# Differential attention: second score product over all 128 rows, with the causal mask as extra rows of it

## The chip, the cores and the metric

One core of one Trainium2 chip. The metric is the device time of one execution in microseconds (us). A core has five engines with instruction queues of their own: TensorE (PE, matrix products; its weight loads are listed apart, as PEld), VectorE (DVE), ScalarE (ACT), GpSimd (POOL) and SyncE (SP), whose queue issues nearly all loads here.

## The reference, cut to what matters

The kernel computes a two-layer encoder trunk for 512 positions and a model width of 1024. The first layer's mixer has two parts side by side, a Mamba-2 scan and a differential attention; only the latter is touched. Eight heads, each with two query/key pairs of width 64, rotary positions, and a block-causal mask of chunks of 64:

```
CHUNK = 64
def chunk_causal_mask(start, seq_len):
    qi = start + jnp.arange(Q_BLOCK, dtype=jnp.int32)
    kj = jnp.arange(seq_len, dtype=jnp.int32)
    return (kj[None, :] // CHUNK) <= (qi[:, None] // CHUNK)
...
    def block(start, q1b, q2b):
        mask = chunk_causal_mask(start, s)
        p1 = masked_softmax(jnp.einsum('bqhd,bkhd->bhqk', q1b, k1, preferred_element_type=F32) * scale, mask)
        p2 = masked_softmax(jnp.einsum('bqhd,bkhd->bhqk', q2b, k2, preferred_element_type=F32) * scale, mask)
        return jnp.einsum('bhqk,bkhe->bqhe', p1 - lam * p2, vf)
```

A block of 128 queries (Q_BLOCK) holds two chunks. Of the keys up to its own end, only one square is masked: the first 64 queries of a block may not see the last 64 keys of it.

## The kernel before, in words

Activations lie transposed, features on the 128 partitions and the 512 positions along the free axis. Every matrix is cut into *units* of 128 output features with up to 1024 inputs. A unit's weights come from HBM on SP's queue (line 157), are split into a rounded high part (ACT, line 169) and the rest (DVE, line 170), both fp32r, and PE adds three products per 128 inputs (lines 178 to 180): 24 products of 128x512 for a full unit, each with a weight load. The raw weights, the split weights and the PSUM tiles of a tag have two buffers each. `drive` (line 244) goes through a list of items, units and small steps; before it computes a unit it prepares the weights of the next.

The order of the list is written out by hand in `even` (lines 886 to 932): the projection dt, then B/C, then x with the rotary tables in steps between (`rope_step`), z with the scan (`pair`), and then the attention. For each head hd the list holds units q, k and v, and between them four stages of the head before: `stage(n)` (line 906) does `flip` of the step two back, `attend` of the step three back and `scores` of step n, where a step is one query block of one head in the order 3, 2, 1, 0 (512, 384, 256, 128 key columns). For odd heads the order is v, stage, stage, q, stage, k, stage; for even heads q, stage, k, stage, stage, v, stage. So the keys of an odd head are followed by one stage and the q unit of the next head before they are scored, those of an even head by more. For heads 4 to 7 a unit of the output projection is put in. During heads 0 and 1 the end of the scan runs beside it: `gate_norm`, `gate_row`, and eight times `gate_split` (line 724: DVE at line 725, ACT at 729, GpSimd at 730).

The list is not the order on the engines: when the program is built, a scheduler of the framework orders the instructions of each engine from it and places the waits. An instruction that depends on nothing can be put far ahead, and products of one unit can stand between those of another step. On the chip each engine then goes through its queue in that fixed order.

`rope` (line 762) turns a projection into rotated q or k on DVE and ACT. `ev_q` (line 776) makes `qa[c]` for component c = 0, 1: the 64 rows `R[c]` hold q rounded to fp32r, the other 64 rows the remainder. `ev_k` (line 787) makes `k1[c]`, the rounded k in both halves, and `k2`, the remainder of k, in the rows `R[c]` of one tile. `scores` (line 800) then takes three products per component: line 812 over 128 rows (rounded q and its remainder, both against rounded k), line 813 over the 64 rows `R[c]` (rounded q against the remainder of k), and line 814 with one row in bf16 (`mrow` against `nrow`, set up in lines 392 to 396), which adds -1e30 to the last 64 columns for the first 64 queries. DVE takes the row maximum (line 815), ACT the exponential with its sum (line 816).

Other names in the text: `k2` (two buffers) also serves as fifth scratch tile of the rotary tables (line 507); `eb0`, `eb1` belong to `pair` and later to `flip` and `attend`; `vt` (two buffers) holds values of heads (line 744).

Of the kernel before, what the change touches and what calls it, by code (L numbers as in the profile page):

```python
# [9 lines left out]
F32 = mybir.dt.float32  # L10
F32R = mybir.dt.float32r
# [7 lines left out]
P = 128  # L19
T = 512  # L20
# [7 lines left out]
NEG = -1.0e30  # L28
# [93 lines left out]
class Trunk:  # L122
# [356 lines left out]
    def even(self, E):  # L479
        nc, a = self.nc, self.a  # L480
        V, A, G, PE = nc.vector, nc.scalar, nc.gpsimd, nc.tensor
# [3 lines left out]
        sp = ssp = None  # L485

        def t2(tag, dt=F32, bufs=None):
            return self.t(sp, [P, T], tag, dt, bufs)

        def sm(tag, w=64, dt=F32, bufs=None):  # L490
            return self.t(ssp, [P, w], "s_" + tag, dt, bufs)
# [7 lines left out]
        def first_norm():  # L499
            E["st"] = self.first_squares([t2(x) for x in ("hs00", "hs01", "hs02", "hs10", "hs11", "hs12", "fx0",  # L500
                                                          "fx1")])
            E["mask"] = sm("mask", P)
            nc.sync.dma_start(out=E["mask"], in_=a["mask"])
            self.norm_done(E)
            self.rope = {n: self.t(self.cp, [P, T], "rope_" + n) for n in ("cos", "sin")}
            tq = [t2("qa0", F32R if i == 2 else F32, 2) for i in range(2)]
            tq += [t2("qa1", F32R if i == 0 else F32, 2) for i in range(2)] + [t2("k2", bufs=2)]
            E["rope"] = self.rope_tables(self.rope["cos"], self.rope["sin"], self.cst("if64"), self.cst("sg64"), tq, True)

        def rope_step():  # L510
# [223 lines left out]
        vt, qs, ks = [None] * 8, [None] * 8, [None] * 8  # L734
# [38 lines left out]

        R = (slice(0, 64), slice(64, 128))

        def ev_q(hd):
            def f_(ps):
                r = rope(ps, 0.125)
                qa = [t2(f"qa{c}", F32R, 2) for c in range(2)]
                for c in range(2):  # L780
                    A.copy(out=qa[c][R[c], :], in_=r[R[c], :])
                    V.tensor_tensor(out=qa[c][R[1 - c], :], in0=r[R[c], :], in1=qa[c][R[c], :].bitcast(F32),
                                    op=ALU.subtract)
                qs[hd] = qa
            return f_

        def ev_k(hd):
            def f_(ps):
                r = rope(ps, 1.0)
                k1 = [t2(f"k1{c}", F32R, 2) for c in range(2)]  # L790
                k2 = t2("k2", F32R, 2)
                for c in range(2):
                    A.copy(out=k1[c][R[c], :], in_=r[R[c], :])
                    A.copy(out=k1[c][R[1 - c], :], in_=r[R[c], :])
                    V.tensor_tensor(out=k2[R[c], :], in0=r[R[c], :], in1=k1[c][R[c], :].bitcast(F32),
                                    op=ALU.subtract)
                ks[hd] = (k1, k2)
            return f_

        def scores(hd, qb):  # L800
            qa, (k1, k2) = qs[hd], ks[hd]
            if qb == 3:
                W["ss", hd] = sm("ss", 8, bufs=2)
            ss = W["ss", hd]
            n = (qb + 1) * P
            qsl = slice(qb * P, (qb + 1) * P)
            nm = sm("nmx", 2, bufs=2)
            pp = W["pp", hd, qb] = [t2(((("md1", "xs7"), ("hs12", "pp1")) if hd > 2 else (("md1", "fx0"), ("fx1", "pp1")))[c][qb % 2])
                                    for c in range(2)]
            for c in range(2):  # L810
                ps = self.ps("sc")
                PE.matmul(ps[:, :n], lhsT=qa[c][:, qsl], rhs=k1[c][:, :n], start=True, stop=False)  # L812
                PE.matmul(ps[:, :n], lhsT=qa[c][R[c], qsl], rhs=k2[R[c], :n], start=False, stop=False)  # L813
                PE.matmul(ps[:, n - 64:n], lhsT=self.mrow, rhs=self.nrow, start=False, stop=True)
                V.tensor_reduce(out=nm[:, c:c + 1], in_=ps[:, :n], axis=AX.X, op=ALU.max, negate=True)
                A.activation(out=pp[c][:, :n], in_=ps[:, :n], func=AF.Exp, bias=nm[:, c:c + 1],
                             accum_out=ss[:, 2 * qb + c:2 * qb + c + 1])
            rr = sm("rr", 1, bufs=2)
            V.reciprocal(out=rr, in_=ss[:, 2 * qb + 1:2 * qb + 2])
            V.scalar_tensor_tensor(out=rr, in0=ss[:, 2 * qb:2 * qb + 1], scalar=E["nlam"], in1=rr, op0=ALU.mult,  # L820
                                   op1=ALU.mult)
            V.scalar_tensor_tensor(out=pp[0][:, :n], in0=pp[1][:, :n], scalar=rr, in1=pp[0][:, :n], op0=ALU.mult,
                                   op1=ALU.add)
# [62 lines left out]
        L = lambda f, *x: (lambda: f(*x))  # L886
        mt = ("mm", "sc")
        ux = self.units("x", 8, xs8, ev_xbc)
        items = [start] + self.units("dt", 1, xs8, ev_dt, tags=mt) + [first_norm]
        items += self.units("bc", 4, xs8, ev_xbc, 1, tags=mt, j0=8)  # L890
        rs = rope_step
        items += ux[:2] + [L(bc_work, 0), rs] + ux[2:3] + [rs] + ux[3:4] + [L(bc_work, 1), rs]
        items += ux[4:5] + [rs] + self.weave(ux[5:], [L(make_xdt, 0, 0), rs] + [L(make_xdt, 0, c) for c in (1, 2, 3)])
        items += [lambda: self.run(E["rope"])]
        uz = self.units("z", 8, xs8, ev_z)
        for i in range(8):
# [643 lines left out]
def pack(i):  # L1540
    i = {k: np.asarray(v) for k, v in i.items()}
    f = np.float32
    par = np.zeros((P, NPAR), f)

    def put(n, v):
        o, w = PAR[n]
        par[:v.shape[0], o:o + w] = v
    put("nm0", _cols(i["norm_mix"][0]))
    put("nm1", _cols(i["norm_mix"][1]))
    put("nf0", _cols(i["norm_ffn"][0]))  # L1550
    put("nf1", _cols(i["norm_ffn"][1]))
    put("nfin", _cols(i["norm_final"]))
    put("gn", _cols(i["ev_gate_norm"][0]))
    put("cw", _cols(i["ev_conv_w"][0]))
    put("cb", _cols(i["ev_conv_b"][0]))
    put("dsk", _cols(np.repeat(i["ev_d_skip"][0], 64)))
    put("sub", _cols(i["ev_subln"][0]))
    put("lam", i["ev_lambdas"][0].T)
    put("qn", _cols(i["od_q_norm"][0]))
    put("kn", _cols(i["od_kv_norm"][0]))  # L1560
    put("bglu", _cols(i["od_b_glu"][0]))
    put("lre", _cols(i["od_lam_re"][0]))
    put("lim", _cols(i["od_lam_im"][0]))
    put("lst", _cols(np.repeat(i["od_log_step"][0], 64)))
    put("d4", np.tile(i["od_d_skip"][0].reshape(16, 32).T, (4, 1)))
    cst = np.zeros((P, NCST), f)

    def putc(n, v):
        o, w = CST[n]
        cst[:, o:o + w] = v  # L1570
    r = np.arange(P)
    putc("ident", np.eye(P))
    mask = (r[:, None] <= r[None, :]).astype(f)
    cidx = np.ascontiguousarray(np.broadcast_to(r[None, :], (P, P))).astype(f)
    if64 = (10000.0 ** (-np.arange(32) * (2.0 / 64))).astype(f)
    if32 = (10000.0 ** (-np.arange(16) * (2.0 / 32))).astype(f)
    putc("if64", if64[r % 32][:, None])
    putc("if32", if32[r % 16][:, None])
    tp = f(2.0 * math.pi)
    putc("sg64", np.where(r % 64 < 32, -tp, tp)[:, None])  # L1580
    putc("sg32", np.where(r % 32 < 16, -tp, tp)[:, None])
    putc("sel", (r[:, None] % 32 == np.arange(16)[None, :]) & (r[:, None] < 64))
    rowp = np.concatenate([i["ev_dt_bias"][0], i["ev_a_log"][0]])[None, :]
    bc = np.concatenate([_t16(i["od_b_re"][0]), _t16(i["od_b_im"][0]),
                         _t16(i["od_c_re"][0].transpose(0, 2, 1)), _t16(i["od_c_im"][0].transpose(0, 2, 1))], axis=1)
    arrays = {"xt": i["x"][0].T, "positions": i["positions"], "par": par, "cst": cst, "mask": mask, "cidx": cidx,
              "rowp": rowp, "s5bc": bc}
    mats = {n: i[n][0] for n in ("ev_w_in", "ev_w_out", "od_w_in", "od_w_glu", "od_w_uq", "od_w_ukv", "od_w_out")}
    for n in ("ffn_gate", "ffn_up", "ffn_down"):
        mats[n + "0"], mats[n + "1"] = i[n]  # L1590
    flat = {}
    for f_, parts in CHUNKS.values():
        flat.setdefault(f_, []).append(np.concatenate(
            [mats[n][k0 * P:(k0 + nk) * P, cc].reshape(nk, P, -1).transpose(1, 0, 2).reshape(P, -1)
             for n, k0, nk, cc in parts], axis=1).ravel())
    for f_, v in flat.items():
        arrays[f_] = np.concatenate(v)
    return {k: np.ascontiguousarray(v) for k, v in arrays.items()}
# [22 lines left out]
```

## Time and profile before

| | before |
|---|---|
| median of 3 runs | 1480.8 us (1479.17 to 1481.18) |
| the profiled execution, its own time | 1481.41 us |
| its span, first to last instruction | 1479.6 us |
| mean granted TensorE clock | 0.986 of 2.4 GHz |
| PE, PEld, DVE, ACT, POOL busy | 96%, 78%, 64%, 45%, 17% |
| instructions | 18488 |

How to read it: busy times of one engine overlap those of the others, and products on PE overlap each other as well, so the start to start distance of two products tells more than their durations. In the timeline a row has the start, the duration, the engine, the line, the operation, output<-inputs, the rows and columns of the weights (for PE), the shape, the count, and in brackets the idle time before it with what ended it. Idle time of an engine that is not on the path costs nothing.

### The profile page before, as it was taken

What the parts mean: (1) busy time and instruction counts of PE and PEld (TensorE: products, weight loads), DVE (VectorE), ACT (ScalarE), POOL (GpSimd) and SP (SyncE); (2) the same over time, 40 slices, a digit from 0 to 9 for tenths busy, and PEclk for the clock granted to TensorE, in tenths of its full rate; (3) what the DMA queues carried; (4) which work ended last, traced back from release to release, by engine and by line L of the source; (5) the groups of instructions that cost most, each with busy time, mean ns of one, the idle gap of its engine ahead of it and who ended that gap; (6) DMA issues with size and microseconds to landing.
All of it is one profiled execution on the core that took longest, in us unless ns stands there. A gap on an engine that the chain in (4) does not pass through costs nothing.

```text
span 1479.6 us, 18488 instructions
## 1 busy us (share of the span) xinstructions
PE 1426.2 (96%) x7043; PEld 1155.1 (78%) x7043; DVE 954.1 (64%) x1992; ACT 661.5 (45%) x1198; POOL 256.9 (17%) x206
## 2 busy tenths in 40 slices
PE   7999999999999999999999997789999999999997
PEld 5877877788878877888888886666688888888887
DVE  6987788777664999774634469886664433443453
ACT  5658766767544334334223453256453322222342
POOL 0234511000002210011011213523221100100111
PEclk9999999999999999999999998889999999999999
DMA  5221121112212222223222221020122232323221
GB/s 179 78 73 58 61 82 44 59 57 72 86 58 85 102 86 86 86 86 107 96 103 87 98 86 38 24 75 2 62 109 85 89 112 86 108 77 114 86 100 57
DMA packets 20248, 119.80 MB, mean 81 GB/s; under 512 B 2368, under 2 KB 3008, under 8 KB 9024
## 3 DMA queue, kind: packets, MB, share of 16 engines
q1 hardware_dynamic: 18864, 116.86, 22.9%
q10 hardware_dynamic: 1296, 1.76, 0.4%
q8 instruction: 55, 0.90, 0.3%
q14 instruction: 33, 0.27, 0.1%
HBM read 116.52 MB, written 2.10 MB: 80 GB/s over the span
## 4 chain that ended last, share of the span: by engine, by line
PE 74%; DVE 18%; ACT 3%; POOL 2%; issue 2%; DMA 1%; SPq 0%; ACTq 0%; DVEq 0%; POOLq 0%
PE mm L178 14%; PE mm L180 14%; PE mm L179 13%; PE sc L180 7%; PE sc L179 7%; PE sc L178 7%; DVE wlo L170 3%; PE sc L1397 1%; PE sc L813 1%; POOL xs L281 1%; PE po L842 1%; DVE qsw L608 1%; PE mm L750 1%; PE po L1425 1%; PE sc L812 1%
## 5 line engine op out<-in xcount | busy, mean ns | idle before, releaser
L169 ACT CAST whi<-raw 128x1024 fp32r<-128x1024 f32 (+5 forms) x231 | 223.9, 970 | 568.6 <-PE mm L179 331.3
L170 DVE TENSOR_TENSOR wlo<-raw,whi 128x1024 fp32r<-128x1024 f32 (+5 forms) x231 | 266.8, 1155 | 44.2 <-ACT whi L169 31.6
L281 POOL TENSOR_TENSOR gt<-gt,rbc 128x512 f32<-128x512 f32 x44 | 76.3, 1734 | 572.6 <-ACT gt L952 572.6
L957 DVE TENSOR_TENSOR gt<-mm,gt 128x512 f32<-128x512 f32 x44 | 30.3, 690 | 111.3 <-PE mm L180 107.9
L281 POOL TENSOR_TENSOR sacc<-sacc,sq 128x512 f32<-128x512 f32 x29 | 45.4, 1566 | 300.5 <-issue 232.7
L951 DVE TENSOR_TENSOR gt<-sc,rbc 128x512 f32<-128x512 f32 x44 | 30.3, 689 | 88.9 <-PE sc L180 88.9
L180 PE MATMUL mm<-x0h,wlo 128*128 128x512 f32 (+2 forms) x91 | 37.2, 409 | 12.4 <-DVE wlo L170 12.4
L178 PE MATMUL mm<-x0h,whi 128*128 128x512 f32 (+2 forms) x91 | 39.9, 438 | 6.1 <-ACT x0h L343 5.4
L972 DVE TENSOR_TENSOR h<-h,mm 128x512 f32<-128x512 f32 x20 | 13.7, 687 | 44.0 <-PE mm L180 44.0
L768 ACT ACTIVATE qsw<-mm 32x512 f32<-32x512 f32 x64 | 37.7, 589 | 3.1 <-DVE qraw L764 2.3
L972 DVE TENSOR_TENSOR h<-h,sc 128x512 f32<-128x512 f32 x20 | 13.7, 686 | 38.9 <-PE sc L180 38.8
L178 PE MATMUL mm<-x1h,whi 128*128 128x512 f32 (+2 forms) x91 | 36.7, 403 | 1.8 <-ACT x1h L343 1.8
L952 ACT ACTIVATE gt<-gt 128x512 f32<-128x512 f32 x44 | 27.6, 628 | 22.9 <-DVE gt L951 22.9
L180 PE MATMUL mm<-x1h,wlo 128*128 128x512 f32 (+2 forms) x91 | 37.3, 410 | 0.0
L180 PE MATMUL mm<-x2h,wlo 128*128 128x512 f32 (+2 forms) x91 | 37.2, 408 | 0.0
L178 PE MATMUL mm<-x7h,whi 128*128 128x512 f32 (+2 forms) x95 | 37.1, 391 | 0.0
L180 PE MATMUL mm<-x7h,wlo 128*128 128x512 f32 (+2 forms) x95 | 37.1, 391 | 0.0
L179 PE MATMUL mm<-x7l,whi 128*128 128x512 f32 (+2 forms) x95 | 37.0, 390 | 0.0
L179 PE MATMUL mm<-x0l,whi 128*128 128x512 f32 (+2 forms) x91 | 36.8, 405 | 0.2 <-DVE x0l L344 0.2
L179 PE MATMUL mm<-x2l,whi 128*128 128x512 f32 (+2 forms) x91 | 37.0, 407 | 0.0
L179 PE MATMUL mm<-x1l,whi 128*128 128x512 f32 (+2 forms) x91 | 36.8, 404 | 0.2 <-DVE x1l L344 0.2
L178 PE MATMUL mm<-x3h,whi 128*128 128x512 f32 (+2 forms) x91 | 36.8, 405 | 0.0
(938 smaller groups left out, 4385.5 us busy)
## 6 DMA issues: line engine op xcount, KB each, us to landing
raw<-in_f_dram SPq DMA_DIRECT2D x52, 1024.0 KB, 4.8
raw<-in_w_dram SPq DMA_DIRECT2D x35, 1024.0 KB, 4.8
raw<-in_f_dram SPq DMA_DIRECT2D x16, 896.0 KB, 4.5
raw<-in_w_dram SPq DMA_DIRECT2D x8, 512.0 KB, 3.6
h<-in_xt_dram SPq DMA_DIRECT2D x8, 256.0 KB, 6.8
raw<-in_w_dram SPq DMA_DIRECT2D x2, 640.0 KB, 3.9
out_dram<-otm SPq DMA_DIRECT2D x4, 256.0 KB, 2.5
out_dram<-otm ACTq DMA_DIRECT2D x4, 256.0 KB, 2.9
```

Of the source, the lines that this page charges most:

```text
L169: nc.scalar.copy(out=hi[:, :n], in_=raw[:, o:o + n])
L170: nc.vector.tensor_tensor(out=lo[:, :n], in0=raw[:, o:o + n], in1=hi[:, :n].bitcast(F32), op=ALU.subtract)
L178: nc.tensor.matmul(ps, lhsT=hi[:, k, :m], rhs=xh, start=start and j == 0, stop=False)
L179: nc.tensor.matmul(ps, lhsT=hi[:, k, :m], rhs=xl, start=False, stop=False)
L180: nc.tensor.matmul(ps, lhsT=lo[:, k, :m], rhs=xh, start=False, stop=stop and j == n - 1)
L281: self.nc.gpsimd.tensor_tensor(out=out, in0=x, in1=y, op=op)
L608: V.scalar_tensor_tensor(out=acc, in0=xr[:, 1 + k:1 + k + T], scalar=self.par("cw", 12 * k + j), in1=acc, op0=ALU.mult, op1=ALU.add)
L768: A.activation(out=sw[c * 32:(c + 1) * 32, :], in_=ps[d * 32:(d + 1) * 32, :], func=AF.Identity, scale=scale)
L951: V.tensor_tensor(out=gt, in0=ps, in1=E["rbc"], op=ALU.mult)
L952: A.activation(out=gt, in_=gt, func=AF.Silu)
L957: V.tensor_tensor(out=gt, in0=ps, in1=gt, op=ALU.mult)
L972: V.tensor_tensor(out=self.h[i], in0=self.h[i], in1=ps, op=ALU.add)
```

## The change

Line 814 and its one-row product are gone. The second product (line 813) becomes one of 128 rows: `q2[c]` against `k2[c]`. In the rows `R[c]` `q2[c]` holds the rounded q (one more ACT copy per component) and `k2[c]` the remainder of k as before, now in a tile of its own for each c. The other 64 rows hold the mask: row b of `q2` is 1 for the first 64 queries of block b, row b of `k2` is -1e30 for the last 64 keys of block b, the remaining rows are zero, so that the product adds -1e30 exactly in the masked squares. These rows are the same for all heads. Eight tiles (`qk2`: q or k, c, even or odd head) keep them, in place of the two buffers of `k2`; a new step `mask_rows`, in the list behind the fifth x unit, fills them once by way of two zeroed tiles of the tag `vt`, four small loads on SP's queue, and eight ACT copies. The host packs the 8x512 table `cmask`. The odd layer's attention keeps its own one-row product.

```diff
-            tq += [t2("qa1", F32R if i == 0 else F32, 2) for i in range(2)] + [t2("k2", bufs=2)]
+            tq += [t2("qa1", F32R if i == 0 else F32, 2) for i in range(2)] + [t2("eb1")]
...
+        def mask_rows():
+            for n in range(2):
+                src = self.t(sp, [P, T], "vt", bufs=2)
+                G.memset(src, 0.0)
+                for c in range(2):
+                    nc.sync.dma_start(out=src[64 * c:64 * c + 4, :], in_=a["cmask"][4 * n:4 * n + 4, :])
+                E["cm", n] = src
+                for c in range(2):
+                    for b in range(2):
+                        x = E["qk2", n, c, b] = t2(f"qk2{n}{c}{b}", F32R)
+                        A.copy(out=x[R[1 - c], :], in_=src[R[1 - c], :])
+
         def ev_q(hd):
...
                 qa = [t2(f"qa{c}", F32R, 2) for c in range(2)]
+                q2 = [E["qk2", 0, c, hd % 2] for c in range(2)]
                 for c in range(2):
                     A.copy(out=qa[c][R[c], :], in_=r[R[c], :])
                     V.tensor_tensor(out=qa[c][R[1 - c], :], in0=r[R[c], :], in1=qa[c][R[c], :].bitcast(F32),
                                     op=ALU.subtract)
-                qs[hd] = qa
+                    A.copy(out=q2[c][R[c], :], in_=r[R[c], :])
+                qs[hd] = qa, q2
...
-                k2 = t2("k2", F32R, 2)
+                k2 = [E["qk2", 1, c, hd % 2] for c in range(2)]
...
-                    V.tensor_tensor(out=k2[R[c], :], in0=r[R[c], :], in1=k1[c][R[c], :].bitcast(F32),
+                    V.tensor_tensor(out=k2[c][R[c], :], in0=r[R[c], :], in1=k1[c][R[c], :].bitcast(F32),
                                     op=ALU.subtract)
...
-                PE.matmul(ps[:, :n], lhsT=qa[c][R[c], qsl], rhs=k2[R[c], :n], start=False, stop=False)
-                PE.matmul(ps[:, n - 64:n], lhsT=self.mrow, rhs=self.nrow, start=False, stop=True)
+                PE.matmul(ps[:, :n], lhsT=q2[c][:, qsl], rhs=k2[c][:, :n], start=False, stop=True)
...
-        items += ux[4:5] + [rs] + self.weave(ux[5:], [L(make_xdt, 0, 0), rs] + [L(make_xdt, 0, c) for c in (1, 2, 3)])
+        items += ux[4:5] + [rs, mask_rows] + self.weave(ux[5:], [L(make_xdt, 0, 0), rs] + [L(make_xdt, 0, c) for c in (1, 2, 3)])
...
+    cm = np.zeros((8, T), f)
+    for b in range(4):
+        cm[b, P * b:P * b + 64] = 1.0
+        cm[4 + b, P * b + 64:P * b + P] = NEG
```

## Rows read from the trace of the kernel before

**Rows 1.** The page, part 1: busy us (share of the span) xinstructions.

```profile
PE 1426.2 (96%) x7043; PEld 1155.1 (78%) x7043; DVE 954.1 (64%) x1992; ACT 661.5 (45%) x1198; POOL 256.9 (17%) x206
```

**Rows 2.** Busy time by stage: length, PE, PEld, DVE, ACT, POOL; clock, DMA share, GB/s.

```profile
189.90:217.60 27.70, 27.21 (x123) 20.83 (x123) 24.29 (x48) 17.64 (x39) 5.54 (x4) 0.94 0.12 41
217.60:237.50 19.90, 16.57 (x72) 12.19 (x69) 19.15 (x27) 15.78 (x34) 5.96 (x4) 0.83 0.15 53
252.10:278.80 26.70, 26.70 (x132) 20.61 (x131) 20.60 (x52) 19.22 (x47) 0.00 (x0) 1.00 0.18 60
278.80:311.50 32.70, 32.70 (x204) 27.90 (x204) 23.35 (x56) 21.32 (x52) 0.00 (x0) 1.00 0.15 49
```

**Rows 3.** The chain that ended last, in the attention: start, us, what.

```profile
221.57 0.66 DVE xs L725
...
237.55 0.39 PE sc L812
```

**Rows 4.** Timeline of PE: scores of 256 columns (head 2), 512 and 384 (head 3).

```profile
262.92 0.36 PE L812 MATMUL sc<-k,qa 128*128 128x256 f32 x1
...
264.41 0.50 PE L178 MATMUL mm<-x0h,whi 128*128 128x512 f32 x1
...
279.20 0.48 PE L812 MATMUL sc<-k,qa 128*128 128x512 f32 x1
279.61 0.49 PE L813 MATMUL sc<-k,qa 64*128 64x512 f32 x1
280.04 0.20 PE L814 MATMUL sc<-nrow,mrow 1*128 1x64 bf16 x1
280.17 0.50 PE L812 MATMUL sc<-k,qa 128*128 128x512 f32 x1
...
281.16 0.50 PE L178 MATMUL mm<-bc,whi 128*128 128x512 f32 x1
281.49 0.40 PE L179 MATMUL mm<-xdt,whi 128*128 128x512 f32 x1
...
281.96 0.40 PE L178 MATMUL mm<-bc,whi 128*128 128x512 f32 x1
...
292.67 0.42 PE L812 MATMUL sc<-k,qa 128*128 128x384 f32 x1
...
294.39 0.66 PE L830 MATMUL tp<-cst,xs 128*128 128x128 f32 x4
```

**Rows 5.** Timeline of the weight loads (PEld) in the same place.

```profile
279.61 0.18 PEld L813 LDWEIGHTS sc<-k,qa 64*128 64x128 f32 x1 [0.24 <-issue]
...
281.50 0.19 PEld L180 LDWEIGHTS mm<-bc,wlo 128*128 128x128 f32 x1
```

**Rows 6.** Timeline of PE: full-height products of 256 and 128 columns, scores of 128.

```profile
299.76 0.28 PE L752 MATMUL mm<-wlo,x0h 128*128 128x256 f32 x1
299.88 0.28 PE L750 MATMUL mm<-whi,x1h 128*128 128x256 f32 x1
...
302.73 1.06 PE L842 MATMUL po<-md,hs 128*128 128x128 f32 x8
303.54 0.30 PE L812 MATMUL sc<-k,qa 128*128 128x128 f32 x1
...
304.80 0.39 PE L750 MATMUL mm<-whi,x4h 128*128 128x256 f32 x1
```

**Rows 7.** Timeline of DVE: the last write of head 3's keys.

```profile
277.20 0.69 DVE L795 TENSOR_TENSOR k<-qraw,k 64x512 fp32r<-64x512 f32 x1
```

**Rows 8.** Line 781 alone: durations in ns, min/median/max; first and last start.

```profile
L781 ACT CAST qa<-qraw x16: 616/619/631, 179.4 to 392.6; 64x512 fp32r<-64x512 f32 x16
```

**Rows 9.** Timeline of GpSimd and of ACT in the first 30 us.

```profile
1.24 0.51 POOL L592 MEMSET pp<- 64x512 f32 x1
...
28.46 1.04 ACT L169 CAST whi<-raw 128x1024 fp32r<-128x1024 f32 x1 [5.35 <-PE mm L179]
```

**Rows 10.** Timeline of PE: the first score product of head 1.

```profile
220.26 0.51 PE L812 MATMUL sc<-k,qa 128*128 128x512 f32 x1 [1.75 <-ACT k L794]
```

More of the change, by code (lines that the diff above doesn't have):

```diff
@@ L800, in scores @@
         def scores(hd, qb):
-            qa, (k1, k2) = qs[hd], ks[hd]
+            (qa, q2), (k1, k2) = qs[hd], ks[hd]
             if qb == 3:
@@ L1586, in pack @@
     arrays = {"xt": i["x"][0].T, "positions": i["positions"], "par": par, "cst": cst, "mask": mask, "cidx": cidx,
-              "rowp": rowp, "s5bc": bc}
+              "rowp": rowp, "s5bc": bc, "cmask": cm}
     mats = {n: i[n][0] for n in ("ev_w_in", "ev_w_out", "od_w_in", "od_w_glu", "od_w_uq", "od_w_ukv", "od_w_out")}
```

## The prediction

> **What bounds the kernel now.** I read the busy shares first: TensorE (PE) works 96% of the span [rows 1], so time leaves this kernel where PE time leaves it, unless another engine is next in line in that stage. Then the busy time by stage over the differential attention, which runs from about 190 to 442 us [rows 2]. Its four columns tell two halves apart. While heads 0 and 1 are scored (the first two rows) VectorE (DVE) is busy 88% and then 96% of the stage, and in the second row PE is down to 16.57 of 19.9 us at a mean granted clock of 0.83 (some of it at 1.2 GHz, the rest at 2.4). From head 2 on PE is busy all the time at full clock, DVE 77% and then 71%, ScalarE (ACT) 72% and then 65%. The chain of waits says the same: at 221.57 us it runs through DVE's gate work (line 725), and it passes over to PE at a score product of head 1, at 237.55 us [rows 3]. So PE time removed before 237.5 us is mostly not on the path, and PE time removed after it is.
>
> **What a score product costs now.** In the order of PE's instructions, start to start is the true price, since durations overlap. One head scores four query blocks (512, 384, 256 and 128 key columns), each for two components c, and each component takes three products: L812 at full height (128 rows), L813 with 64 rows, L814 with one row. For 512 columns L813 starts 0.41 us after L812, L814 0.43 us after that, and the next product 0.13 us after L814 [rows 4]. A full-height product of the same width takes 0.235 us (281.49 to 281.96, two of them), so it is not the columns that take 0.43 us. The weight loads show what does: L813's load starts at 279.61, together with its own product and after the one before, while the load of the full-height L180 runs from 281.50 to 281.69, under the L179 that started at 281.49 [rows 5]. Every step from one height to another leaves a load uncovered. It is paid three times per component: into L813, into L814, and into the product behind it, which takes 0.33 us instead of 0.235 (281.16 to 281.49).
>
> **Part 1: the products (lines 812 to 814).** Before, for both components with the 0.10 us of the late load behind: 512 columns, 279.20 to 281.16, 1.96 + 0.10 = 2.06 us; 384, 292.67 to 294.39, 1.82; 256, 262.92 to 264.41, 1.59 [rows 4]; 128, 303.54 to 304.80, 1.36 [rows 6]. That is 6.83 us a head. After: four full-height products per block, with one geometry all through. 512 costs 0.235 each; 256 costs 0.12 (299.76 to 299.88); 128 costs 0.10 (eight of L842 from 302.73 to 303.54) [rows 6]; for 384 no row stands alone, so I take 0.18, an estimate halfway between 0.12 and 0.235. Sum 4 x (0.235 + 0.18 + 0.12 + 0.10) = 2.54 us. So 4.29 us a head leave PE. Head 1's last two blocks (2.95 - 0.88 = 2.07) and heads 2 to 7 (25.7) lie behind 237.5 us: **27.8 us**. Head 0 and the first half of head 1 hold the other 6.5.
>
> **What of it lies on the path.** Heads 3 to 7 (21.4 us): a period such as 278.8 to 311.5 shrinks from 32.7 to 28.4 us, with DVE 23.35 and ACT 21.32 + 1.24 in it, 82% and 79% [rows 2]. The first stage in rows 2 shows PE at 98% busy beside a DVE at 88%, so I let these savings stand, but for one place. In odd heads the scores follow closely on their keys: DVE's last write of head 3's k ends at 277.89 [rows 7], and its first score product starts at 279.20 [rows 4], 1.31 us of cover. The last scores of the head before lie between, and they get 0.96 us shorter, so a slip of half a microsecond in DVE's queue now stalls PE: 0.5 us at each of three odd heads, 1.5 in all. Head 2 and the end of head 1 (6.4 us): the period of 26.7 us falls to 22.4, with DVE 20.60 (92%) and ACT 20.5 (91%), between the 88% at which PE was still full and the 96% at which it was not; I take three quarters, 4.8. Heads 0 and 1, before 237.5 us: bounds 0 and 6.5. The first stage could shrink by about 2.4 us until DVE is at the 96% of the second, the second not at all; I take 1.0.
>
> **Part 2: two more ACT copies per head (q2 from r).** 16 casts of 64x512 like L781, 0.62 us each [rows 8]: 9.9 us of ACT, behind PE work in heads 2 to 7 (already counted in the 1.24 above). In ACT's queue the first of them stands ahead of the cast for c = 1, so DVE's subtraction at line 782 comes 0.62 us later; scores of a head come a whole unit and more after its q. In heads 0 and 1 ACT is on the DVE-bound chain in places: bounds 0 and 2.5 us (four copies), I take 0.5, as ACT has 4 us free in the second stage of rows 2. If that cover goes, the price is the 2.5.
>
> **Part 3: the mask step.** Two memsets on GpSimd, four small loads on SP's queue, eight ACT casts (5.0 us by the same row). The order on the engines is the scheduler's, not the program's: the memset of line 592, which the program reaches six projection units after the first, ran at 1.24 us [rows 9]. The new memsets depend on nothing and should go there too, the loads behind those of x on SP, past which only weight loads stand, and the casts into an early hole of ACT such as the 5.35 us before 28.46 us, where ACT only waits for PE to give a weight buffer back [rows 9]. I take 0. If they fall amid busy ACT work instead, up to 5.0 us of weight splits come later; below 0 nothing speaks for a gain. Replacing k2 by eb1 in the table scratch moves no instruction.
>
> **Sum.** 21.4 - 1.5 + 4.8 + 1.0 - 0.5 - 0 = 25.2 us. The profiled execution took 1481.41 us (span 1479.6 plus 1.8 around it), so 1456.2; the median shown is 0.6 us lower. Forecast: 1455.6 us.
>
> **The rivals.**
> *The early heads gain too.* If DVE's gate work merely follows PE there, all 34.3 us come back: 1446.5. The 96% of DVE in rows 2 and the chain in rows 3 speak against it.
> *DVE and ACT take over.* The chain from keys or softmax to the next PE step, not the busy share, limits heads 2 to 7, and half of the 27.8 is lost in waits: 1467. For it: the 1.75 us that PE waited for head 1's keys [rows 10]. Against it: no such wait in the full rows of rows 2.
> *A full-height load is not hidden either.* If a load hid only under a product of other rows, the new second product would still take its 0.43 us and only L814's 0.13 us (280.04 to 280.17) would go: 52 x 0.13 = 6.8 us, 1474. The Trainium skill's page "TensorE: Matmul & The Clock Gate", Part 3, says that a weight load overlaps a running product only when the row group differs. The trace disagrees: the load under L179 [rows 5] and 0.12 us at 256 columns.
> *Slower.* PE out of work at every handover from keys to scores. The stage at 217.6 us shows what one costs: 3.3 us idle (19.9 - 16.57) and 17% of 16.57, 2.8 us, to the lower clock, 6.1 us. It outweighs the gain from the fifth of the six heads 2 to 7; at all six it is 36.6 against 27.8, 1490. It needs a DVE that falls behind for good; even heads have had a whole unit of work between keys and scores, so I see little for it.
> *Nothing comes of it,* because the removed time was not on the path at all: 1480.
>
> **How the numbers follow.** Forecast case 0.68, early heads 0.10, DVE and ACT 0.13, the load 0.04, slower 0.03, nothing 0.02. The range reaches from the full saving (1447) to the half one (1468), which leaves out the last three cases and some of each edge. A change of 0.2%, 3 us, is what a measurement of this kernel can tell from none. Faster takes all cases but the last two, less a little for both sides: 0.94; within 0.2% 0.02; slower 0.04.
>
> **What would show it.** L812 and the new second product 0.235 us apart at 512 columns, no load that starts with its own product, the product behind at its usual pace; attention over some 25 us earlier; PE idle in heads 0 and 1 higher than before by 4 to 6 us; waits of PE for k or q tiles at odd heads short. The mechanism is wrong if the second product keeps 0.43 us; the path is wrong if PE's idle time in heads 2 to 7 grows by more than 5 us; the mask step is mispriced if weight products before 40 us start later.

## The result, and the profile after

The changed kernel took 1457.06 us (median of four, 1456.46 to 1457.81) against 1480.03 us before: ratio 0.9845, 95% interval 0.9828 to 0.9862, 23 us faster. The forecast was 1455.6. The profiled execution took 1457.81 us, 23.6 less than that of before.

The page's first part, busy us by engine, beside [rows 1]:

```profile
PE 1395.0 (96%) x6979; PEld 1142.9 (78%) x6979; DVE 950.5 (65%) x1992; ACT 674.0 (46%) x1222; POOL 257.3 (18%) x208
```

PE lost 31 us of busy time and stayed at 96%; ACT gained 12.5 us. The 23.6 us are placed by stage, cut where the same instruction starts in both traces: at the first score product, at head 1's third block (where the chain passes to PE, [rows 3]), and at DVE's last gate product of the attention. Busy time by stage, columns as in [rows 2], of before:

```profile
189.90:237.55 47.65, 43.78 (x193) 33.02 (x192) 43.47 (x74) 33.47 (x72) 11.50 (x8) 0.89 0.14 46
237.55:441.00 203.45, 203.45 (x1113) 165.81 (x1114) 144.93 (x364) 125.11 (x309) 0.00 (x0) 1.00 0.20 68
```

and of after:

```profile
187.74:232.72 44.98, 36.99 (x181) 30.01 (x180) 41.00 (x74) 34.06 (x74) 7.69 (x6) 0.92 0.13 48
232.72:415.50 182.78, 180.02 (x1063) 157.33 (x1062) 144.23 (x364) 132.13 (x322) 3.06 (x2) 1.00 0.22 76
```

In the second stage, from head 1's third block to the end of head 7, PE was never idle before; it now has 23.4 us less busy time (203.45 to 180.02) and 2.8 us of waits, so the stage is 20.7 us shorter. In the first stage PE has 6.8 us less busy time, but DVE is busy for 91% of it, and the chain that ended last runs there mostly through DVE and through ACT's rope copies (line 768): PE's idle time rises from 3.9 to 8.0 us, and 2.7 us come back. Another 2.2 us were ahead before the first score (189.92 to 187.74), and of the 25.5 us at the end of the attention 1.9 were lost again by the end. Those last two numbers belong to the execution and not to the kernel, and the 2.7 is no fixed number, as the section on the steps shows: 2.2 + 2.7 + 20.7 - 1.9 = 23.6 with rounding.

The scores themselves, timeline of PE after, heads 4 (512 columns) and 3 (384):

```profile
300.16 0.48 PE L828 MATMUL sc<-k,qa 128*128 128x512 f32 x1
300.48 0.40 PE L829 MATMUL sc<-qk,qk 128*128 128x512 f32 x1
300.71 0.39 PE L828 MATMUL sc<-k,qa 128*128 128x512 f32 x1
300.94 0.39 PE L829 MATMUL sc<-qk,qk 128*128 128x512 f32 x1
301.17 0.27 PE L845 MATMUL tp<-cst,md 128*128 128x128 f32 x1
```

```profile
282.90 0.42 PE L828 MATMUL sc<-k,qa 128*128 128x384 f32 x1
283.16 0.34 PE L829 MATMUL sc<-qk,qk 128*128 128x384 f32 x1
283.33 0.34 PE L828 MATMUL sc<-k,qa 128*128 128x384 f32 x1
283.51 0.34 PE L829 MATMUL sc<-qk,qk 128*128 128x384 f32 x1
283.68 0.60 PE L845 MATMUL tp<-cst,xs 128*128 128x128 f32 x4
```

In the second component line 829 runs 0.23 us after line 828 at 512 columns (0.32 in the first, whose line 828 enters late behind 128-column products), where line 813 had stood 0.41 and line 814 another 0.43 behind [rows 4]. Its load shows what changed. The timeline of the weight loads at the same place:

```profile
300.25 0.19 PEld L829 LDWEIGHTS sc<-qk,qk 128*128 128x128 f32 x1
300.48 0.19 PEld L828 LDWEIGHTS sc<-k,qa 128*128 128x128 f32 x1
```

The load at 300.25 starts while line 828's product runs and is over before its own product's start at 300.48; that of line 813 had started only with its own product, 0.41 us after the product ahead [rows 4, rows 5].

What is late now: PE's waits in the attention after, from 185 to 418 us (engine, line and what it waited for; us in total, times, longest).

```profile
PE po L857 <- ACT s_junk L860: 3.1, 4, 1.4
PE sc L828 <- ACT k L810: 2.8, 2, 2.4
PE mm L178 <- DVE vt L758: 2.1, 1, 2.1
PE sc L829 <- DVE qk L811: 2.0, 2, 1.9
```

The first row is new. How it comes about in head 3, the timeline of PE and then of ACT:

```profile
286.51 0.49 PE L857 MATMUL po<-md,eb 128*128 128x128 f32 x2 [0.68 <-ACT s_junk L860]
```

```profile
283.68 2.39 ACT L768 ACTIVATE qsw<-mm 32x512 f32<-32x512 f32 x4
286.09 0.28 ACT L860 ACTIVATE s_junk<-po 128x128 f32<-128x128 f32 x1
```

ACT's square of one attended block reads the PSUM tile into which PE writes the next block. In odd heads four rope copies of the next keys or queries (2.39 us) stand ahead of that square in ACT's queue. PE now comes to its next block early enough to wait for it.

### The profile page after: what moved, and what is told of

Read it like the earlier page. It is cut to its first block, busy times and chain, and to the rows that moved or that the text cites. A ratio compares the mean times of both kernels' runs of the same rounds, so it can differ in the third digit from the quotient of the medians.

```text
span 1456.0 us, 18392 instructions
## 1 busy us (share of the span) xinstructions
PE 1395.0 (96%) x6979; PEld 1142.9 (78%) x6979; DVE 950.5 (65%) x1992; ACT 674.0 (46%) x1222; POOL 257.3 (18%) x208
## 4 chain that ended last, share of the span: by engine, by line
PE 69%; DVE 20%; ACT 6%; issue 2%; POOL 2%; DMA 1%; SPq 0%; ACTq 0%; DVEq 0%; POOLq 0%
PE mm L178 13%; PE mm L179 13%; PE mm L180 13%; PE sc L180 7%; PE sc L179 7%; PE sc L178 7%; DVE wlo L170 3%; DVE qsw L608 2%; ACT qsw L768 1%; PE sc L1412 1%; ACT whi L169 1%; POOL xs L281 1%; PE po L1440 1%; PE po L857 1%; PE tp L1430 1%
## 5 line engine op out<-in xcount | busy, mean ns | idle before, releaser
L178 PE MATMUL mm<-x0h,whi 128*128 128x512 f32 (+2 forms) x91 | 38.9, 428 | 8.2 <-ACT x0h L343 6.0
L179 PE MATMUL mm<-x2l,whi 128*128 128x512 f32 (+2 forms) x91 | 37.1, 407 | 0.0
L178 PE MATMUL mm<-x7h,whi 128*128 128x512 f32 (+2 forms) x95 | 37.1, 390 | 0.0
L179 PE MATMUL mm<-x7l,whi 128*128 128x512 f32 (+2 forms) x95 | 37.0, 389 | 0.0
L178 PE MATMUL mm<-x1h,whi 128*128 128x512 f32 (+2 forms) x91 | 36.5, 401 | 0.3 <-ACT x1h L343 0.3
L179 PE MATMUL mm<-x0l,whi 128*128 128x512 f32 (+2 forms) x91 | 36.6, 402 | 0.2 <-DVE x0l L344 0.2
L178 PE MATMUL mm<-x2h,whi 128*128 128x512 f32 (+2 forms) x91 | 36.7, 404 | 0.0
L179 PE MATMUL mm<-x1l,whi 128*128 128x512 f32 (+2 forms) x91 | 36.4, 400 | 0.2 <-DVE x1l L344 0.2
```

The source lines that it names most:

```text
L178: nc.tensor.matmul(ps, lhsT=hi[:, k, :m], rhs=xh, start=start and j == 0, stop=False)
L179: nc.tensor.matmul(ps, lhsT=hi[:, k, :m], rhs=xl, start=False, stop=False)
```

## The experiments

Twelve kernels ran. Where a diff has no other name, it is against the changed kernel.

**The mask step alone.** Scores as before, with their 64-row and one-row products; the mask rows are still made.

```diff
-                    A.copy(out=q2[c][R[c], :], in_=r[R[c], :])
...
-                k2 = [E["qk2", 1, c, hd % 2] for c in range(2)]
+                k2 = [E["qk2", 1, 0, hd % 2]] * 2
...
-                PE.matmul(ps[:, :n], lhsT=q2[c][:, qsl], rhs=k2[c][:, :n], start=False, stop=True)
+                PE.matmul(ps[:, :n], lhsT=qa[c][R[c], qsl], rhs=k2[c][R[c], :n], start=False, stop=False)
+                PE.matmul(ps[:, n - 64:n], lhsT=self.mrow, rhs=self.nrow, start=False, stop=True)
```

> The mask step (two memsets, four loads, eight ACT casts, the eight tiles, the scratch tile exchanged) is in, but the scores take their three products as before, with the 64-row and the one-row product. Theory: the step falls into holes and costs nothing, 1480 us within 1.5. Rival: the 2.2 us by which the changed kernel is early at its first score product come from this step and the new order of the work around it, so they show here as well, 1478 us at the first score and at the end.

Measured: 1480.16 us, ratio to before 1.0001 [0.9989, 1.0012]. The step costs nothing that a measurement can tell. The timeline of ACT in the changed kernel shows where its eight casts lie:

```profile
18.66 2.29 ACT L788 CAST qk<-vt 64x512 fp32r<-64x512 f32 x4
...
21.92 2.29 ACT L788 CAST qk<-vt 64x512 fp32r<-64x512 f32 x4
26.94 1.04 ACT L169 CAST whi<-raw 128x1024 fp32r<-128x1024 f32 x1 [2.73 <-PE mm L179]
```

They lie in two holes in which ACT waits for PE to give a weight buffer back, 2.66 and 5.35 us long before (the second in [rows 9]); 2.73 us of the second are left.

**Full height, with the one-row product put back behind.**

```diff
-                PE.matmul(ps[:, :n], lhsT=q2[c][:, qsl], rhs=k2[c][:, :n], start=False, stop=True)
+                PE.matmul(ps[:, :n], lhsT=q2[c][:, qsl], rhs=k2[c][:, :n], start=False, stop=False)
+                PE.matmul(ps[:, n - 64:n], lhsT=self.mrow, rhs=self.nrow, start=False, stop=True)
```

> The changed kernel, but the one-row mask product (line 814 of before) is put back behind the full-height product; the mask is then added twice, which leaves the softmax as it is. Theory (a load is uncovered at each change of height): the way into the one-row product costs 0.19 us, the product 0.13, the late load behind it 0.10, together 0.42 us in each of 64, of which 52 lie where PE is the bound: 22 us less the quarter that the changed kernel also lost of its PE savings, so 1457 + 17 = 1474 us (1471 to 1478). Rival (the 64-row product is slow by itself, as half the array stands idle): only 52 x 0.13 = 6.8 us come back, 1464 us.

Measured: 1469.06 us, ratio 0.9931 [0.9914, 0.9948], 12 us over the changed kernel, between the two numbers and below the theory's 1471 to 1478. Timeline of PE:

```profile
305.48 0.40 PE L829 MATMUL sc<-qk,qk 128*128 128x512 f32 x1
305.81 0.20 PE L830 MATMUL sc<-nrow,mrow 1*128 1x64 bf16 x1
305.94 0.50 PE L828 MATMUL sc<-k,qa 128*128 128x512 f32 x1
306.27 0.40 PE L829 MATMUL sc<-qk,qk 128*128 128x512 f32 x1
```

and of its loads:

```profile
305.80 0.09 PEld L830 LDWEIGHTS <-mrow 1*128 1x128 bf16 x1 [0.36 <-issue]
```

The one-row product delays itself by 0.10 (0.33 instead of 0.23 behind line 829), takes 0.13, and delays the product behind by 0.10. The theory had put 0.19 on the way in, the length of a load of 64 or 128 rows. The one-row load is 0.09 us long and starts with its own product, so it lies in the 0.13; what fills the 0.10 ahead of it these rows do not show. With the measured term, 52 x 0.33 = 17 us by three quarters gives the 12 to 13 us measured.

**The one-row product left out of the kernel before.** Line 814 goes, the 64-row product stays; the causal mask inside the diagonal blocks is left out.

```diff
-                PE.matmul(ps[:, :n], lhsT=qa[c][R[c], qsl], rhs=k2[R[c], :n], start=False, stop=False)
-                PE.matmul(ps[:, n - 64:n], lhsT=self.mrow, rhs=self.nrow, start=False, stop=True)
+                PE.matmul(ps[:, :n], lhsT=qa[c][R[c], qsl], rhs=k2[R[c], :n], start=False, stop=True)
```

> The kernel before, but without the one-row product: the mask is left out, so that all keys of a block are seen. Theory (changes of height): two changes are left of three per component, 0.23 us go in each, 52 x 0.23 = 12 us of PE, 9 to 12 on the path: 1468 to 1471 us, and the 64-row product still stands 0.43 us from its neighbours at 512 columns. Rival (a 64-row product is slow by itself): 0.13 each, 6.8 us, 1473 us. If the two parts were independent, the gains of this run and of the run with the one-row product put back would add up to the 23 us of the change; by the theory they add up to less, as a change of height goes only when both products are full.

Measured: 1472.44 us, ratio 0.9955 [0.9941, 0.9970], 7.6 us faster than before and 15 slower than the change. Timeline of PE:

```profile
306.45 0.49 PE L813 MATMUL sc<-k,qa 64*128 64x512 f32 x1
306.88 0.50 PE L812 MATMUL sc<-k,qa 128*128 128x512 f32 x1
307.31 0.50 PE L813 MATMUL sc<-k,qa 64*128 64x512 f32 x1
307.74 0.33 PE L829 MATMUL tp<-cst,md 128*128 128x128 f32 x1
```

The time misses the theory's 1468 to 1471 and lies by the rival's 1473: two products of a component now take 0.86 us where three took 0.99, so the one-row product was worth its own 0.13 and no more. The rival itself does not fit the rows, though: line 812 has its full height here too and still takes 0.43 us between 64-row products, where the same product of the changed kernel (line 828) takes 0.23 between full ones. The steps 128 to 64 and 64 to 128 rows are both left, at 0.43 us each. So the halves don't add up: one (putting the second product to full height) gave 11.0 us, the other 7.6, both together 23. The price hangs on the steps between heights, and only both edits together leave none.

**The one-row product padded with zeros to 128 rows**, in the kernel of the second experiment, where the mask is added twice.

```diff
-        self.mrow = self.t(cp, [1, P], "mrow", BF16)
+        self.mfull = self.t(cp, [P, P], "mrow", BF16)
+        nc.gpsimd.memset(self.mfull, 0.0)
...
-                PE.matmul(ps[:, n - 64:n], lhsT=self.mrow, rhs=self.nrow, start=False, stop=True)
+                PE.matmul(ps[:, n - 64:n], lhsT=self.mfull, rhs=self.nfull, start=False, stop=True)
```

> The changed kernel with the old mask product behind the two others took 1469.1 us, 12 more than the changed kernel: 52 products, each with 0.10 us for the way in, 0.13 for itself and 0.10 for the way back. Here that product is padded with zeros from one row to 128 rows. Theory: the price is the height, not the product: the ways in and back go, and 52 products of 64 columns cost about 0.10 us each, three quarters of it on the path, 4 us: 1461 us, 1459 to 1464. Rival: a third product costs its place in the row whatever its height: 1469 us, 1467 to 1471. The mask is added twice here, as in that run.

Measured: 1462.00 us, ratio 0.9881 [0.9866, 0.9896]. Timeline of PE:

```profile
301.38 0.40 PE L832 MATMUL sc<-qk,qk 128*128 128x512 f32 x1
301.61 0.20 PE L833 MATMUL sc<-nrow,mrow 128*128 128x64 bf16 x1
301.65 0.48 PE L831 MATMUL sc<-k,qa 128*128 128x512 f32 x1
301.97 0.40 PE L832 MATMUL sc<-qk,qk 128*128 128x512 f32 x1
```

and of its loads:

```profile
301.61 0.10 PEld L833 LDWEIGHTS <-mrow 128*128 128x128 bf16 x1 [0.27 <-issue]
301.62 0.20 PEld L831 LDWEIGHTS sc<-k,qa 128*128 128x128 f32 x1
```

The same number of products, 127 rows of zeros more, and 7 us less: 0.23 into the product instead of 0.33, and 0.04 for it instead of 0.13. What is left, 0.09 at the product behind (0.32 instead of 0.23), falls where two loads of 0.10 and 0.20 us have 0.04 us of work to cover them; I take them for its reason. The padded product's load also starts only with its own product, and yet nothing is lost ahead of it: that sign alone does not tell an uncovered load, the distance between products does. Against the second experiment only the height of this product changes, so the pair shows most cleanly that the height sets the price.

**The changed kernel once more, and the q2 casts.** The changed kernel ran again unaltered, without the two casts per head (the product of the rounded q with the remainder of k is left out), with them on GpSimd, and with the squares of heads 0 to 6 gathered at the end of each head.

```diff
+                        if n == 0:
+                            G.memset(x[R[c], :].bitcast(F32), 0.0)
...
-                    A.copy(out=q2[c][R[c], :], in_=r[R[c], :])
```

```diff
-                    A.copy(out=q2[c][R[c], :], in_=r[R[c], :])
+                    G.tensor_copy(out=q2[c][R[c], :], in_=r[R[c], :])
```

```diff
-            A.activation(out=junk[:, 0:P], in_=po[:, qsl], func=AF.Square, accum_out=s2[:, qb:qb + 1])
+            for b in ((3, 2, 1, 0) if hd < 7 and qb == 0 else () if hd < 7 else (qb,)):
+                A.activation(out=junk[:, 0:P], in_=po[:, b * P:(b + 1) * P], func=AF.Square,
+                             accum_out=s2[:, b:b + 1])
```

> The changed kernel once more, unaltered. 1457 us within 1. If the 2.4 us that its profile lost in the odd layer (products at 1.2 GHz behind a wait of 4.4 us, where the kernel before had them at 2.4) and the 1.2 us that it won in the first 20 us belong to the kernel, they show again; if they are a matter of the single execution, one or both are gone.

> The changed kernel without the two ACT casts per head that write the rounded q into q2; these rows are zeroed once instead, so that the product of rounded q with the remainder of k is left out. PE's products are the same. Theory: the casts hide, apart from some 0.5 us in heads 0 and 1: 1456 to 1457 us. Rival: ACT's 9.9 us of casts are what kept the saving in heads 2 to 7 at 20.7 instead of 27.8 us; then some 4 to 6 us come back, 1452 us.

> The changed kernel with the two casts per head moved from ACT to GpSimd, which has nothing to do in heads 2 to 7. Theory: no difference beyond 1 us, 1456 to 1458 us, as neither is on the path. Rival as in the run without the casts: 1452 us. Slower by some us if GpSimd's copies are late in heads 0 and 1, where it works on the gate.

> The changed kernel, with the four squares per head that ACT takes of the attention output (line 860) moved to the end of the head for heads 0 to 6, so that PE's next block of the output need not wait for ACT's read of the one before. Theory: the waits of 0.68 us in heads 3 and 5 and 1.38 in head 1 were made by ACT's four rope copies standing ahead of the square; without them PE gains 1.5 to 2 us, 1455 us. Rival: ACT is as late for the softmax, and the wait only moves to the transposes or the scores: 1457 us.

Measured, ratios to the same runs of before (1479.57 us): unaltered 1458.76 (1456 to 1458 was expected), 0.9854 [0.9834, 0.9874]; no casts 1457.83, 0.9852 [0.9831, 0.9872]; casts on GpSimd 1458.16, 0.9848 [0.9829, 0.9867]; squares at the head's end 1460.34, 0.9862 [0.9839, 0.9884]. Leaving 9.9 us of ACT out gains nothing in the whole time, to within 3 us. The traces tell more. From head 2's first score product to DVE's last gate product of the attention, the changed kernel takes 168.73 us, the kernel without the casts 168.02 and the one with the casts on GpSimd 168.36, while the five other executions with the same attention code lie between 168.75 and 168.84. So the casts cost 0.4 to 0.7 us there and are otherwise hidden. The squares are no way to more. PE's waits in that last kernel, same stretch and columns as above:

```profile
PE sc L828 <- ACT k L810: 3.0, 1, 3.0
PE sc L829 <- DVE qk L811: 2.8, 1, 2.8
...
PE sc L828 <- ACT md L831: 2.0, 3, 0.7
...
PE po L857 <- ACT s_junk L861: 0.4, 1, 0.4
```

The wait for the square falls from 3.1 to 0.4 us, and the others grow from 7.8 to 11.8 us together: the wait only moves.

**The same idea in the odd layer's attention.** There a score product of 96 rows was followed by the same one-row mask product. The mask goes into rows 96 to 99 of q and k, by sixteen more ACT copies and two loads.

```diff
+                    A.copy(out=x[hh][96:100, :], in_=E["cm5", n][96:100, :])
...
-                PE.matmul(ps[:, :n], lhsT=qk[m][0][hh][0:96, qb * P:(qb + 1) * P], rhs=qk[m][1][hh][0:96, :n],
-                          start=True, stop=False)
-                PE.matmul(ps[:, n - 64:n], lhsT=self.mrow, rhs=self.nrow, start=False, stop=True)
+                PE.matmul(ps[:, :n], lhsT=qk[m][0][hh][0:100, qb * P:(qb + 1) * P], rhs=qk[m][1][hh][0:100, :n],
+                          start=True, stop=True)
```

> The changed kernel, and in the odd layer's attention the mask as rows 96 to 99 of the one score product there (96 rows before), its 32 one-row products gone; 16 small ACT casts of four rows and two small loads more. Theory (changes of height): each one-row product costs its 0.13 us, an uncovered load of 0.2 before it and 0.1 behind it, 32 x 0.43 = 13.8 us in a stage where PE is busy 65 of 65 us, three quarters of it on the path: 1447 us (1443 to 1451). Rival (only the one-row product itself goes, since a 96-row product already uses another height than its neighbours): 32 x 0.13 = 4.2 us, 1453 us. Other rival: the 16 casts hold up ACT, and nothing is won, 1457 us.

Measured: 1449.11 us, ratio to before 0.9800 [0.9786, 0.9815], and 8 us faster than the changed kernel: of the kernels that compute the whole reference in its own precision this and the next are the fastest. Its score products still stood 0.43 us apart at 512 columns, which I read as loads left uncovered at less than full height, and padded them:

```diff
-                    A.copy(out=x[hh][96:100, :], in_=E["cm5", n][96:100, :])
+                    A.copy(out=x[hh][96:128, :], in_=E["cm5", n][96:128, :])
...
-                PE.matmul(ps[:, :n], lhsT=qk[m][0][hh][0:100, qb * P:(qb + 1) * P], rhs=qk[m][1][hh][0:100, :n],
+                PE.matmul(ps[:, :n], lhsT=qk[m][0][hh][:, qb * P:(qb + 1) * P], rhs=qk[m][1][hh][:, :n],
```

> The run before this one in the same layer (score product over 100 rows, mask in rows 96 to 99) took 1449.1 us, and its score products still stand 0.36 to 0.43 us apart at 512 columns although all are equally high; a load of 0.19 us starts only when the product before it is done. Here the same products reach over all 128 rows, rows 100 to 127 zeros. Theory: what a load needs to lie under the product before it is the full height, not a height equal to its neighbour's: the four passes of a block and the product behind them fall to 0.235, 0.18, 0.12 and 0.11 us apart by columns, from 2.05 to 1.18 us a block at 512 and 8.6 us over the 16 blocks, nearly all on the path: 1441 us, 1439 to 1444. Rival: equal height is enough and the 0.43 us are something else of these products (their two passes): no change, 1449 us, 1447 to 1451.

Measured: 1448.55 us, ratio 0.9794 [0.9778, 0.9811]: no change; the theory fell. The loads in the run with 100 rows say why, at 512 columns and then at 256 (timeline of the weight loads):

```profile
1004.47 0.19 PEld L1416 LDWEIGHTS sc<-rc,b 100*128 100x128 f32 x1 [0.24 <-issue]
1004.90 0.19 PEld L178 LDWEIGHTS mm<-t,whi 128*128 128x128 f32 x1 [0.24 <-issue]
1005.33 0.19 PEld L179 LDWEIGHTS mm<-hr,whi 128*128 128x128 f32 x1 [0.24 <-issue]
...
1015.21 0.19 PEld L178 LDWEIGHTS mm<-cq0h,whi 128*128 128x128 f32 x1
1015.43 0.19 PEld L179 LDWEIGHTS mm<-cq0l,whi 128*128 128x128 f32 x1
```

One load starts as each product begins, one ahead of its own. L178's at 1004.90 and L179's at 1005.33 bracket the last score pass: 0.43 us at 512 columns, 0.22 at 256. That goes by columns, with no fixed part, so these passes are slow and their loads hidden. An uncovered load has a fixed part: line 813's 64-row product before took 0.26, 0.31, 0.37 and 0.43 us at 128 to 512 columns (means over 52 products, to the next start), 0.06 per 128 columns on top of some 0.19, the length of its load. What the odd layer's products have instead is fp32 tiles, where the differential attention has fp32r. Two runs with fp32r tiles, the part of q and k below its rounding left out, with 100 rows and with 128:

```diff
-                x = qk[m][n] = [t5(f"{('b1', 'rc')[n]}{2 * (m % 2) + hh}") for hh in range(2)]
+                x = qk[m][n] = [t5(f"{('b1', 'rc')[n]}{2 * (m % 2) + hh}", F32R) for hh in range(2)]
```

> The odd layer's score products of the last run stood 0.43 us apart at 512 columns even at full height, so height is not what keeps their loads of 0.19 us uncovered. What they have and the differential attention's products have not is fp32 tiles, for which the profile records two passes per product. Here the run with 100 rows has its q and k tiles in fp32r: one pass per product, and the part of q and k below fp32r's rounding is left out. Theory A (the two passes leave the load uncovered, and among one-pass products equal height is enough): the second product of a block 0.235 us after the first at 512 columns, a block of 512 down from 2.05 to 0.71 us, 13 us in all: 1436 us. Theory B (beside that, a product must reach over all 128 rows): 0.43 us between the two, 0.43 to the product behind, about 9 us in all: 1440 us. Rival C (something else of this place): as B here, and 0.43 us in the next run too.

> The same with the products padded to 128 rows of fp32r; again the part of q and k below fp32r's rounding is left out. Theories A and B: 0.235 us from the first product of a block to the second at 512 columns and 13 us less than the run in fp32: 1436 us (1433 to 1440). Rival C: 0.43 us between them, 1440 us. Between A and B this run is the same; the run with 100 rows tells them apart.

Measured in one execution each: 1444.81 and 1446.63 us (before 1478.42 beside them). Timeline of PE with 100 rows:

```profile
997.73 0.28 PE L1416 MATMUL sc<-rc,b 100*128 100x256 f32 x1
997.85 0.39 PE L179 MATMUL mm<-u,whi 128*128 128x512 f32 x1
...
1004.45 0.40 PE L1416 MATMUL sc<-rc,b 100*128 100x512 f32 x1
1004.69 0.60 PE L1433 MATMUL tp<-cst,rs 128*128 128x128 f32 x4
```

A 100-row product between 128-row ones takes 0.12 us at 256 columns and 0.24 at 512, as a full one does: from 100 to 128 rows there is no step. Theory A held in the products and missed the time by 9 to 11 us: from 955 to 985 us PE is busy 25.8 of 30 us (27.5 with fp32 tiles), waiting 2.4 us for a weight cast and 1.5 us for the softmax, and its mean granted clock is 0.77 from 985 to 1000 us (1.00 with fp32 tiles). So much of the PE time freed there was not on the path; how much the lower clock took was not measured.

## Why the prediction was right, step by step

The mechanism held at each mark that the prediction had set: second product 0.23 us behind the first, its load under it, the product behind at its usual pace, the attention 25.5 us earlier at its end (25 forecast, but 2.2 of it were ahead at its start), PE idle in heads 0 and 1 up by 4.1 us (4 to 6), and in the rest by 2.8 (under 5); no weight product before 40 us came more than 0.6 us later. One reading was too strong: line 812's recorded end, 279.68, lies behind line 813's load at 279.61 and is modelled, so the rows show a load that starts with its own product, not one that starts after the product before. What shows it uncovered is the fixed 0.19 us at every width. The terms were less exact than their sum.

- **PE time behind 237.5 us: 27.8 forecast, 23.4 measured.** This is the step that was mis-sized. Summed over all score products from PE's starts, waits left out, before took 40.4 us where my blocks gave 41.3 (the 2.6 us of late loads not counted); after takes 18.3 where I had 16.1, since a full-height product costs 0.26, 0.20, 0.13 and 0.125 us in its place, not 0.235, 0.18, 0.12 and 0.10: the first of a block often enters late (0.32 at 300.16). That is 22.1 us where the sum had 25.2. The products behind gave back 2.7 us, as forecast (2.6; from 0.34 to 0.24 us each where they have 512 columns). The other products of the stage took 1.4 us more than before, in small amounts at products that enter late; the sum had no term for that, and its reason stays open.
- **Waits behind 237.5 us: 1.5 + 1.6 forecast, 2.8 measured.** Size right, place half wrong. The keys of head 3 cost 0.40 us, as feared; the larger part is ACT's square behind the rope copies, which I had not looked for: I had followed DVE's queue to the keys and not ACT's to the PSUM tile.
- **Heads 0 and 1: 1.0 - 0.5 forecast, 2.7 in the profiled execution.** This is no fixed number, and that it came out above the forecast is luck. The unaltered kernel's other profiled execution took for its two stages

```profile
189.16:237.03 47.87, 39.46 (x181) 32.15 (x180) 41.40 (x74) 34.52 (x76) 7.69 (x6) 0.85 0.13 45
237.03:420.29 183.26, 180.89 (x1062) 158.33 (x1062) 144.06 (x363) 131.88 (x320) 3.14 (x2) 0.99 0.22 75
```

  against 44.98 and 182.78 us above. The second stage is 0.5 us longer, and its granted clock 0.99 and not 1.00. From head 2's first score product on it repeats to 0.02 us, first in the profile of after and then in this execution:

```profile
246.78:415.51 168.73, 166.57 (x953) 144.22 (x952) 132.97 (x327) 120.79 (x293) 0.00 (x0) 1.00 0.22 76
251.54:420.29 168.75, 166.56 (x953) 144.20 (x952) 132.99 (x326) 120.81 (x293) 0.00 (x0) 1.00 0.22 76
```

  The first stage is as long as before the change (47.65), at a mean granted clock of 0.85 and not 0.92 (more of it at 1.2 GHz, less at 2.4), with PE idle for 8.4 us and not 8.0. So the early heads gave 2.7 and -0.2 us in two executions of one kernel; with the scores as before it varies too (46.60 us in the run with the mask step alone). Why the clock differs from one to the other stays open.
- **Casts and mask step: 0.5 and 0.** The mask step is hidden, as its own run showed. The casts cost 0.4 to 0.7 us, but from head 2 on, where the sum had put nothing; in heads 0 and 1, where it had put the 0.5, the executions differ by more than that.
- **Outside the attention: 0 forecast, 2.2 - 1.9 measured, neither the kernel's.** The first score starts between 187.0 and 191.5 us in the executions of the changed kernel and its variants, at 189.9 before the change, and at 187.9 in the kernel before without its one-row product. The loss behind lies in the odd layer, between ACT's 140th and 144th weight cast: 33.8 us in the profile of before and 36.1 in that of after, but 33.8 in the unaltered kernel's second execution and 36.1 in the run with the mask step alone. It has two values whatever the kernel. In the longer one PE waits 4.4 us for an ACT result (line 1379), in the shorter 1.7, at nearly the same granted clock (0.91 and 0.90); why stays open.

So the saving behind 237.5 us was 4.0 us short (24.7 to 20.7). In this execution the early heads (2.2 over their forecast) and what lies outside the attention (0.3) made 2.5 of that good, by luck and not by the kernel. The rivals: DVE and ACT do take their part, but 2.8 us of it and not 13.9. A full-height load does hide, as the load at 300.25 shows; the Trainium skill's rule that the prediction cites for that rival does not hold here. The lower clock that the slower case needs is missing: from 232.72 us to the end of the attention the granted clock is 1.00 in the profile of after.

Another page bears on this. The Trainium skill's page "TensorEngine Tiling (Array Packing)", section "Tiling Modes", lists modes of 128, 64 and 32 rows and says that changing the mode drains TensorE. The runs fit it. They show 0.19 us at a step between 128 and 64 rows, 0.10 into a one-row product, and nothing between 100 and 128. That a drain is what costs was only inferred; what the traces show is a load that starts only with its own product, and a fixed part as long as that load. No run has 64-row products behind one another.

## What to carry to other kernels

Read PE's true prices from start to start, and look for products that stand further apart than others of the same width and type, with a load that starts only with its own product: here a small product between tall ones cost its own load and delayed its neighbours. Fold it into spare rows of a tall product, or pad it with zeros; remove every such step at once, since here either half alone gave less than half of the gain (11.0 and 7.6 of 23 us). Before calling a load uncovered, compare two widths: a fixed part as long as the load points to the load, a time that goes by columns to the product itself. And when PE is freed, follow each engine's queue to the buffers that PE writes into, not only to the data it reads.

## What the runs showed of the hardware that was not expected

- Adding 127 rows of zeros to a one-row product made it cheaper: 0.04 us in its place and 0.23 into it, where one row took 0.13 and 0.33, and 7 us in the kernel.
- A pass over fp32 tiles took 0.43 us at 512 columns and 0.22 at 256, and the profile records two passes per product (64 for 32 products), so an fp32 product costs nearly four times an fp32r product of the same width (0.86 to 0.235 us). The Trainium skill's page "FP8 and Floating Point Precision", "TensorE Precision Notes", speaks of four passes for true FP32. The records show two, each at nearly twice the time of an fp32r pass.
- The same kernel's stage with heads 0 and 1, where DVE is busiest, differed by 2.9 us between two executions (47.87 and 44.98), with the granted clock 0.85 and 0.92, while from head 2 on, where PE is the bound, the two agreed to 0.02 us.
